# The compression's narrow products between the values' products: one at a time, two behind every three, from the fifth chunk on

## The chip, the cores and the metric

The program runs on one core of a Trainium2 chip, as one launch. The metric is the device time of the whole program in microseconds (us). Before the change the median of three runs is 3626.85 us (3621.54 to 3629.15). A core has a matrix engine (TensorE, PE in the rows), a vector engine (VectorE, DVE), an engine for activation functions and copies (ScalarE, ACT), a general engine (GpSimd, POOL) and one that issues transfers (SyncE, SP). Each works through its own list of instructions in the order of that list; an instruction waits until what it reads is there and the buffer it writes is free.

## The reference

Sequence 512, width 1024, fp32. The first block has two layers, each a feed-forward part, a mixer and a second feed-forward part; a second block (pooling and attention mixers, squared-ReLU MLPs, with a context of 256) follows. The change is in the mixer of the first block, which runs twice, once a layer:

```python
z = n @ mix_w_in[l]                      # queries, keys/values, gates, u and v
y_a = _nsa(q, k_cmp, v_cmp, k_sel, v_sel, k_win, v_win, gates, pe, w1, w2)
y_b = _gmlp(zuv, ln_g, ln_b, ws, bs)

def compress(t, j):                      # in _nsa: 31 windows of 32 positions
    blk = t[:, win_idx] + pe[j][None, None, :, None, :]
    h = jax.nn.silu(jnp.einsum('bnlgd,ldf->bngf', blk, w1[j]))
    return h @ w2[j]
...
kc = _rope(compress(k_cmp, 0), ccos, csin);  vc = compress(v_cmp, 1)
# o = gate0 * attention over kc/vc + gate1 * selected blocks + gate2 * window

def _gmlp(uv, ln_g, ln_b, ws, bs):
    u, v = jnp.split(jax.nn.gelu(uv), 2, axis=-1)
    v = _layernorm(v, ln_g, ln_b)
    ...                                  # chunks of 128 positions, 8 groups
    sv = jnp.einsum('gts,bnsgc->bntgc', w, v) + bs.T[None, None, :, :, None]
    return u * sv.reshape(B, S, GM_WIDTH)
```

## The kernel before

Dense products keep fp32 precision by splitting each operand into a high part and a rest: ScalarE makes the high part of a weight (`whi`, L98), VectorE or GpSimd the rest (`wlo`, L100), and three products are summed (`mm3`, L114 to L116). Weights arrive as raw tiles of 128 x 1024 in three buffers.

In `mix_body` the mixer goes as follows.

- **Queries and keys of group 0**: products (512 wide), rotation (`rotate`, L669 reads the product's PSUM buffer), and the split into high part and rest: `qs` (L688) on VectorE, `kk` by ScalarE (L699), VectorE (L701) and GpSimd (L702).
- **Values** (`values`): eight chunks k of the 1024 inputs, and for each chunk four blocks i of 128 tokens; each of these 32 places is one `mm3` with 280 columns (L114 to L116, `128x280`), into four PSUM buffers, two of the pool `s` and two of the pool `mm`.
- **Compression** (`compress(0)` for keys, `compress(1)` for values): 16 products each of 62 columns over the raw keys or values, `aux<-B,raw` at L761, the narrow products; behind them tanh, the product with w2 (L771 for keys, L786 for values), the rotation of the compressed key (L774 to L778, its sum is `kc`) and its transposition (L780).
- **gMLP, v** (`tok_proj`, L654 to L656, 256 wide, weights from `mix_gv`), gelu (L913, L915), layernorm (L925 to L935, result `vln`).
- **Attention**, group by group: scores against the compressed keys (L832, 16 products of 64 columns) and a softmax in `pcm` (L836); then scores (L815, L816, mask L869), softmax `p` (L873 to L882), transpositions (L886, L891), products with the values (L854, L855), and sums `yv` (L898, L899).
- **Queries and keys of group 1**, and the **spatial gating**: u (gelu), products `ws` x `vln` (L959).

`values` and `compress` are generators. The loop at L797 runs the values, which yield once per chunk, and from chunk `CMP_FROM` = 2 on adds `CMP_RATE` = 1.5 to an account, from which whole steps of the compression are taken; a step of the compression is four narrow products (it yields where q % 4 == 3). What remains runs behind the loop (`run_steps(cmp)`).

What is written so is not the last word on the order: a scheduler then lists each engine's instructions anew by its own estimates of when their operands are ready, within the limits of the pools' buffers. So gv products stand among the values and the attention, and products of group 1 (the fill in the text below) among the steps of the attention of group 0.

Of the kernel before, what the change touches and what calls it, by code (L numbers as in the profile page):

```python
# [32 lines left out]
GELU_A = 0.044715  # L33
GELU_B = 0.7978845608028654
WINDOWS = (2, 4, 8, 16)
CMP_FROM, CMP_RATE = 2, 1.5
BAND = 144
WEAVE = (2, 3, 3, 1.65, 3)

# [12 lines left out]
def build(tc, d, stop=99):  # L52
# [27 lines left out]
    def pc(name, off=0, n=8):  # L80
        o = PCOLS[name] + off
        return par[:, o:o + n]
# [5 lines left out]
    def psum(pool_=None, tag="mm"):  # L88
        return (pool_ or cur["mm"]).tile([128, 512], F32, name=tag, tag=tag)

    def wload(src, F=1024):
        raw = wraw_p.tile([128, 1024], F32, name="raw", tag="raw")
        SY.dma_start(raw[:, :F], src)
        return raw[:, :F]
# [8 lines left out]
    def wget(src, F=1024, eng=None):  # L103
        return wsplit(wload(src, F), F, eng)

    def split(hi, lo, src, eng=None):
        A.activation(hi, src, AF.Copy)  # L107
        (eng or V).tensor_tensor(lo, src, hi, op=OP.subtract)  # L108
# [4 lines left out]
    def mm3(ps, lh, ll, rh, rl, start, stop):  # L113
        T.matmul(ps, lh, rh, start=start, stop=False)  # L114
        T.matmul(ps, lh, rl, start=False, stop=False)  # L115
        T.matmul(ps, ll, rh, start=False, stop=stop)  # L116
# [70 lines left out]
    def modcols(mods, g, jsh, jsc):  # L187

        gs = small.tile([128, 8], F32, name="gs", tag="gs", bufs=4)
        V.scalar_tensor_tensor(gs, mods[:, jsc * 8:(jsc + 1) * 8], 1.0, g, op0=OP.add, op1=OP.mult)  # L190
        return gs, mods[:, jsh * 8:(jsh + 1) * 8]
# [239 lines left out]
    def run_steps(gen, n=None):  # L431
        if gen is None:
            return
        i = 0
        for _ in gen:
            i += 1
            if n is not None and i >= n:
                return

    def chain(*gens):  # L440
        for g in gens:
            yield from g
# [143 lines left out]
    def mixer(l, mods, pre, tail):  # L586
        with ExitStack() as st:
            mix_body(l, mods, pre, tail, st)

    def mix_body(l, mods, pre, tail, st):  # L590
# [14 lines left out]
        def t2(name, shape=(128, S)):  # L605
            return tmp.tile(list(shape), F32, name=name, tag="t2")
# [133 lines left out]
        def values(pss):  # L740
            for k0, kn in ((0, 3), (3, 3), (6, 2)):
                hi, lo = wget(d["mix_v"][l, :, k0 * 280:(k0 + kn) * 280], kn * 280)
                for kk in range(kn):
                    k = k0 + kk
                    w0, w1 = hi[:, kk * 280:(kk + 1) * 280], lo[:, kk * 280:(kk + 1) * 280]
                    for i in range(4):
                        sl = slice(i * 128, (i + 1) * 128)
                        mm3(pss[i][:, 0:280], nhi(k)[:, sl], nlo(k)[:, sl], w0, w1, k == 0, k == 7)
                    yield

        w2s = mc.tile([128, 2, HD], F32, name="w2", tag="w2")
        SY.dma_start(w2s, d["cmp_w2"][l].rearrange("j p e -> p j e"))
# [1 line left out]
        def compress(j):  # L754
            B, w2 = KV_BLOCKS[j], w2s[:, j]
            hp = psum(aux, "aux")
            hv = hp[:, 0:62].rearrange("p (g n) -> p g n", g=NG)
            for w in range(2):
                w1 = wload(d["cmp_w1"][l, j, w])
                for q in range(8):  # L760
                    T.matmul(hv, w1[:, q * 128:(q + 1) * 128], B[:, 8 * w + q, :, 0:NCMP], start=w + q == 0, stop=w * q == 7)  # L761
                    if q % 4 == 3:
                        yield
            z = hp[:, 0:62]
            th = mc.tile([128, 62], F32, name="zth", tag="zth")
            A.activation(th, z, AF.Tanh, scale=0.5)
            sv = mc.tile([128, 62], F32, name="sv", tag="sv")
            V.scalar_tensor_tensor(sv, th, 1.0, z, op0=OP.add, op1=OP.mult)
            if j == 0:
                kp = psum(aux, "aux")  # L770
                T.matmul(kp[0:62, 0:HD], sv, w2, start=True, stop=True)  # L771
                ta, tb, kc = t2("kt1", (62, HD)), t2("kt2", (62, HD)), t2("kc", (62, 2, HD))
                V.tensor_tensor(ta, kp[0:62, 0:HD], ropec[:, 0], op=OP.mult)
                V.tensor_tensor(tb.rearrange("p (j e) -> p j e", j=2),  # L774
                                kp[0:62, 0:HD].rearrange("p (j e) -> p j e", j=2)[:, ::-1, :],
                                ropec[:, 1].rearrange("p (j e) -> p j e", j=2), op=OP.mult)
                for e in range(2):
                    V.tensor_tensor(kc[:, e], ta, tb, op=OP.add)  # L778
                tp = psum(aux, "aux")
                T.transpose(tp[:, 0:62], kc.rearrange("p e d -> p (e d)"), ident[0:62, 0:62])  # L780
                tv = tp[:, 0:62].rearrange("p (g n) -> p g n", g=NG)
                split(KC[:, 0, :, 0:NCMP], KC[:, 1, :, 0:NCMP], tv)
            else:
                vp = psum(aux, "aux")
                for g in range(NG):
                    T.matmul(vp[0:NCMP, g * HD:(g + 1) * HD], sv[:, g * NCMP:(g + 1) * NCMP], w2,  # L786
                             start=True, stop=True)
                vf = t2("vf", (NCMP, NG, HD))
                V.tensor_scalar(vf, vp[0:NCMP, 0:128].rearrange("p (g e) -> p g e", g=NG), 0.5, None,
                                op0=OP.mult)  # L790
                split(VC[0:NCMP, :, 0], VC[0:NCMP, :, 1], vf)
            yield

        pss = [psum(s_p, "s") if i < 2 else psum() for i in range(4)]
        cmp = chain(compress(0), compress(1))
        acc = 0.0
        for k, _ in enumerate(values(pss)):  # L797
            if k >= CMP_FROM:
                acc += CMP_RATE
                run_steps(cmp, int(acc)) if acc >= 1 else None  # L800
                acc -= int(acc)
        for i in range(4):
            split(VV[:, i, :, 0], VV[:, i, :, 1], pss[i][:, 0:256].rearrange("p (c e) -> p c e", c=4))
            A.activation(gth[:, i], pss[i][:, 256:280], AF.Tanh, scale=0.5)
# [662 lines left out]
    with ExitStack() as st:  # L1467
# [3 lines left out]
        with ExitStack() as ist:  # L1471
# [29 lines left out]
            gs, _ = modcols(ml1, pc("g_mix_pre_2", 8), 0, 1)  # L1501
# [120 lines left out]
            for u in (0, 1, 4, 2, 3, 5):  # L1622
                own = first_tiles(u) if u < 2 else None
                pss = [x[:, 0:256] for x in own] if own else tok_proj(d["qkv"][u], u > 3)
# [222 lines left out]
```

## Time and profile before

| | |
|---|---|
| median of three runs | 3626.85 us |
| the profiled execution's own time | 3629.45 us |
| its span in the trace | 3627.7 us |
| instructions in the span | 44600 |
| mean granted TensorE clock, share of full | 0.979 |
| TensorE busy | 3472.6 us (96%) |
| VectorE busy | 2299.2 us (63%) |
| ScalarE busy | 1462.9 us (40%) |
| GpSimd busy | 476.0 us (13%) |

Busy shares are over the whole span. The granted clock is a share of full speed, 2.4 GHz; 0.5 is the lower level, 1.2 GHz. In rows of the timeline a matmul's start is the useful column: the matmuls are pipelined, so a row's duration overlaps the next one, and the step from start to start is what a product takes of the engine. The first mixer of the two lies at about 390 to 680 us, the second at about 1540 to 1830.

### The profile page before, as it was taken

To read this page: it belongs to the slowest core of one execution; us is meant where nothing else is said; L and a number is where in the kernel's file an instruction comes from. 1 tells how busy PE (TensorE), PEld (TensorE's weight loads), DVE (VectorE), ACT (ScalarE), POOL (GpSimd) and SP (SyncE) were. 2 spreads that over 40 slices of the span, in tenths; PEclk is the share of its full clock that TensorE was granted. 3 is DMA by queue.
4 is the path that set the end of the run, shared out by engine and by line. 5 is a ranking of instruction groups with operands and counts; after the bars stand their busy time and mean duration, and the time that the engine had idled before them with its cause. 6 is when DMAs were issued, how large, how long until landed. Compare 5 with 4: busy or idle time off the path is not lost.

```text
span 3627.7 us, 44600 instructions
## 1 busy us (share of the span) xinstructions
PE 3472.6 (96%) x16924; PEld 2861.7 (79%) x16924; DVE 2299.2 (63%) x3715; ACT 1462.9 (40%) x2487; POOL 476.0 (13%) x470
## 2 busy tenths in 40 slices
PE   7999999999999999999999999979999988989998
PEld 5788886788878888887688888868888877767886
DVE  8863677458753996378636966675445578654434
ACT  4222475433223422257624224654433435634232
POOL 4020113021000303022104020210000021130000
PEclk9999999999999999999999999989999999999999
DMA  6862221236862475231123763314444421013332
GB/s 237 287 235 92 95 77 48 69 103 240 292 210 91 156 244 171 88 109 51 44 88 133 248 234 99 108 56 134 128 130 127 133 66 59 1 47 99 97 96 70
DMA packets 140985, 461.55 MB, mean 127 GB/s; under 512 B 16869, under 2 KB 19297, under 8 KB 140641
## 3 DMA queue, kind: packets, MB, share of 16 engines
q1 hardware_dynamic: 140768, 458.69, 38.9%
q8 instruction: 133, 2.18, 0.2%
q14 instruction: 84, 0.68, 0.1%
HBM read 456.53 MB, written 2.10 MB: 126 GB/s over the span
## 4 chain that ended last, share of the span: by engine, by line
PE 63%; DVE 7%; ACT 2%; issue 1%; POOL 1%; DMA 1%; SPq 0%; DVEq 0%; ACTq 0%; POOLq 0%
PE mm L114 18%; PE mm L116 18%; PE mm L115 18%; DVE nt L200 1%; DVE wlo L100 1%; PE mm L324 1%; PE aux L1665 1%; PE aux L886 1%; DVE h L1108 0%; DVE n L206 0%; PE o L854 0%; ACT whi L98 0%; DVE ssum L150 0%; POOL shp L215 0%; PE o L115 0%
## 5 line engine op out<-in xcount | busy, mean ns | idle before, releaser
L98 ACT ACTIVATE whi<-raw 128x1024 fp32r<-128x1024 f32 (+2 forms) x636 | 619.3, 976 | 1469.1 <-PE mm L115 1075.0
L100 DVE TENSOR_TENSOR wlo<-raw,whi 128x1024 fp32r<-128x1024 f32 (+3 forms) x605 | 694.7, 1150 | 506.9 <-ACT whi L98 499.0
L114 PE MATMUL mm<-n,whi 128*128 128x512 f32 x2096 | 831.5, 397 | 14.2 <-ACT nt L202 9.2
L116 PE MATMUL mm<-n,wlo 128*128 128x512 f32 x2096 | 824.6, 394 | 4.3 <-DVE wlo L100 4.1
L115 PE MATMUL mm<-n,whi 128*128 128x512 f32 x2096 | 822.8, 393 | 0.4 <-DVE n L206 0.2
L114 PEld LDWEIGHTS mm<-n,whi 128*128 128x128 f32 x2096 | 395.8, 189 | 98.4 <-issue 11.3
L116 PEld LDWEIGHTS mm<-n,wlo 128*128 128x128 f32 x2096 | 395.3, 189 | 95.7 <-DVE wlo L100 7.3
L115 PEld LDWEIGHTS mm<-n,whi 128*128 128x128 f32 x2096 | 395.7, 189 | 85.2 <-DVE n L206 0.9
L423 DVE SCALAR_TENSOR_TENSOR junk<-adaw,crow 128x1024 f32<-128x1024 f32 x288 | 353.3, 1227 | 76.7 <-DMA adaw<-adaT 59.3
L114 PE MATMUL mm<-r,whi 128*128 128x512 f32 x976 | 385.5, 396 | 4.6 <-ACT r L254 3.1
L116 PE MATMUL mm<-r,wlo 128*128 128x512 f32 x976 | 385.1, 395 | 0.1
L115 PE MATMUL mm<-r,whi 128*128 128x512 f32 x976 | 382.3, 392 | 0.2 <-DVE r L108 0.2
L114 PEld LDWEIGHTS mm<-r,whi 128*128 128x128 f32 x976 | 183.6, 188 | 44.4 <-ACT r L254 4.0
L116 PEld LDWEIGHTS mm<-r,wlo 128*128 128x128 f32 x976 | 183.9, 188 | 43.0 <-DVE wlo L100 0.8
L115 PEld LDWEIGHTS mm<-r,whi 128*128 128x128 f32 x976 | 184.0, 189 | 41.6 <-DVE r L108 0.5
L114 PE MATMUL mm<-hid,whi 128*128 128x512 f32 x448 | 176.7, 394 | 0.0
L116 PE MATMUL mm<-hid,wlo 128*128 128x512 f32 x448 | 175.7, 392 | 0.0
L115 PE MATMUL mm<-hid,whi 128*128 128x512 f32 x448 | 174.7, 390 | 0.0
L563 DVE SCALAR_TENSOR_TENSOR h<-mm,hg,h 128x512 f32<-128x512 f32 x96 | 71.9, 749 | 118.5 <-PE mm L116 118.2
L150 POOL TENSOR_TENSOR ssum<-ssum,sq 128x512 f32<-128x512 f32 x27 | 40.6, 1504 | 778.2 <-ACT sq L149 778.2
L545 DVE TENSOR_TENSOR hd<-mm,sil 128x512 f32<-128x512 f32 x79 | 54.4, 688 | 116.0 <-PE mm L116 115.7
L108 DVE TENSOR_TENSOR ptl<-aux,pth 128x512 fp32r<-128x512 f32 x144 | 94.7, 684 | 43.8 <-ACT pth L107 43.2
(500 smaller groups left out, 5808.3 us busy)
## 6 DMA issues: line engine op xcount, KB each, us to landing
adaw<-adaT SPq DMA_DIRECT2D x240, 512.0 KB, 4.8
raw<-ffn_in SPq DMA_DIRECT2D x170, 512.0 KB, 4.6
raw<-mlp_in SPq DMA_DIRECT2D x96, 512.0 KB, 3.8
raw<-ffn_out SPq DMA_DIRECT2D x64, 512.0 KB, 4.3
raw<-mlp_out SPq DMA_DIRECT2D x64, 512.0 KB, 3.8
raw<-mlp_out SPq DMA_DIRECT2D x64, 256.0 KB, 2.9
raw<-ffn_out SPq DMA_DIRECT2D x32, 384.0 KB, 3.1
raw<-mix_zb SPq DMA_DIRECT2D x16, 512.0 KB, 3.6
```

Of the source, the lines that this page charges most:

```text
L98: A.activation(hi[:, :F], raw, AF.Copy)
L100: (eng or cur["lo"]).tensor_tensor(lo[:, :F], raw, hi[:, :F], op=OP.subtract)
L108: (eng or V).tensor_tensor(lo, src, hi, op=OP.subtract)
L114: T.matmul(ps, lh, rh, start=start, stop=False)
L115: T.matmul(ps, lh, rl, start=False, stop=False)
L116: T.matmul(ps, ll, rh, start=False, stop=stop)
L150: self.last = (eng or V).tensor_tensor(self.acc, self.acc, sq, op=OP.add)
L200: V.scalar_tensor_tensor(t, src[:, k], gs[:, k:k + 1], bc, op0=OP.mult, op1=OP.mult)
L324: T.matmul(self.pss[n], w[:, sl], x, start=k + e == 0, stop=k == DC - 1 and e == 2)
L423: V.scalar_tensor_tensor(junk, w, 1.0, cs[v], op0=OP.mult, op1=OP.mult, accum_out=mods[v][:, j * 8 + m:j * 8 + m + 1])
L545: V.tensor_tensor(hd, pss[1], sil, op=OP.mult)
L563: V.scalar_tensor_tensor(h[:, m], ps, hg[:, m:m + 1], h[:, m], op0=OP.mult, op1=OP.add)
```

## The change

The values yield after every `mm3`, so 32 times, and hand out the chunk's number; the compression yields after every narrow product; and from the chunk of index 4 on, two steps of the compression are taken after each `mm3`. The account goes. From L799 on, the new file's lines are 2 to 3 lower than the old one's.

```diff
-CMP_FROM, CMP_RATE = 2, 1.5
+CMP_FROM, CMP_RATE = 4, 2
...
                     for i in range(4):
                         sl = slice(i * 128, (i + 1) * 128)
                         mm3(pss[i][:, 0:280], nhi(k)[:, sl], nlo(k)[:, sl], w0, w1, k == 0, k == 7)
-                    yield
+                        yield k
...
                     T.matmul(hv, w1[:, q * 128:(q + 1) * 128], B[:, 8 * w + q, :, 0:NCMP], start=w + q == 0, stop=w * q == 7)
-                    if q % 4 == 3:
-                        yield
+                    yield
...
         cmp = chain(compress(0), compress(1))
-        acc = 0.0
-        for k, _ in enumerate(values(pss)):
+
+        for k in values(pss):
             if k >= CMP_FROM:
-                acc += CMP_RATE
-                run_steps(cmp, int(acc)) if acc >= 1 else None
-                acc -= int(acc)
+                run_steps(cmp, CMP_RATE)
```

In TensorE's order of before, a layer's 32 narrow products stand as a block of 8 at the start of the values, two blocks of 4 among them, and a block of 16 behind them. This is the stretch between the two blocks of 4, one whole chunk of the values (`n_3011`, `n_3012` are the normed input's high part and rest, `B` the raw keys or values with the positions' offsets):

```order
L761 MATMUL aux<-B,raw 128x62 x4
L114 MATMUL s<-whi,n_3011 128x280
L115 MATMUL s<-wlo,n_3011 128x280
L116 MATMUL s<-whi,n_3012 128x280
...
L114 MATMUL mm<-whi,n_3011 128x280
L115 MATMUL mm<-wlo,n_3011 128x280
L116 MATMUL mm<-whi,n_3012 128x280
L761 MATMUL aux<-B,raw 128x62 x4
```

And this is TensorE's order of the changed kernel, where the values' fifth chunk stands:

```order
L116 MATMUL s<-whi,n_3012 128x280
L761 MATMUL aux<-B,raw 128x62 x2
L114 MATMUL s<-whi,n_3011 128x280
L115 MATMUL s<-wlo,n_3011 128x280
L116 MATMUL s<-whi,n_3012 128x280
L761 MATMUL aux<-B,raw 128x62 x2
L114 MATMUL mm<-whi,n_3011 128x280
L115 MATMUL mm<-wlo,n_3011 128x280
L116 MATMUL mm<-whi,n_3012 128x280
L761 MATMUL aux<-B,raw 128x62 x2
```

The two blocks of 4 have become four pairs, each behind three products; the blocks of 8 and of 16 are as before.

At the end of the values TensorE had, before (`n_3011` and `n_3012` are the normed input's high part and rest, `kc__3197` the compressed keys, `qs_3235` the queries of group 0, `sv` the compression's hidden layer):

```order
L654 MATMUL mm<-whi,n_3011 128x256
L780 MATMUL aux<-ident,kc 128x62
L761 MATMUL aux<-B,raw 128x62 x16
L655 MATMUL mm<-wlo,n_3011 128x256
L656 MATMUL mm<-whi,n_3012 128x256
L654 MATMUL mm<-whi,n_3011 128x256
L655 MATMUL mm<-wlo,n_3011 128x256
L832 MATMUL s<-kc__3197,qs_3235 128x64 x8
L786 MATMUL aux<-w_3321,sv 31x64 x2
L832 MATMUL s<-kc__3197,qs_3235 128x64 x8
L656 MATMUL mm<-whi,n_3012 128x256
```

and has in the changed kernel (lines up to 3 lower):

```order
L116 MATMUL mm<-whi,n_3012 128x280
L779 MATMUL aux<-ident,kc 128x62
L761 MATMUL aux<-B,raw 128x62 x16
L829 MATMUL s<-kc__3197,qs_3235 128x64 x5
L785 MATMUL aux<-w_3321,sv 31x64 x2
L829 MATMUL s<-kc__3197,qs_3235 128x64 x11
L654 MATMUL mm<-whi,n_3011 128x256
L655 MATMUL mm<-wlo,n_3011 128x256
L812 MATMUL s<-kk_3268,qs_3235 128x128
```

No gv product stands between the values and the compressed scores any more; they have moved behind these, and two of them instead of ten stand ahead of the first score of the attention. On VectorE the first copy of the keys (L701) has moved ahead of the sum of the compressed key (L778); on ScalarE and GpSimd the copies of the keys have moved ahead of the first gv weights' parts.

Behind the attention of group 0, TensorE had before (`n_3011`, `n_3012` as above, `vln_4200` and `vln_4201` the normed v; the product that the gating interrupts is one for group 1):

```order
L116 MATMUL mm<-n_3011,wlo 128x512
L959 MATMUL mm<-ws,vln_4200 64x128 x2
L959 MATMUL mm<-ws,vln_4201 64x128 x2
L959 MATMUL mm<-ws,vln_4200 64x128 x2
L959 MATMUL mm<-ws,vln_4201 64x128 x2
L114 MATMUL mm<-n_3011,whi 128x512
```

and has in the changed kernel:

```order
L829 MATMUL s<-kc__3197,qs_4522 128x64 x7
L956 MATMUL mm<-ws,vln_4200 64x128
L114 MATMUL mm<-n_3011,whi 128x512
L115 MATMUL mm<-n_3012,whi 128x512
L956 MATMUL mm<-ws,vln_4200 64x128
L116 MATMUL mm<-n_3011,wlo 128x512
L114 MATMUL mm<-n_3011,whi 128x512
L956 MATMUL mm<-ws,vln_4201 64x128
L115 MATMUL mm<-n_3012,whi 128x512
L116 MATMUL mm<-n_3011,wlo 128x512
L956 MATMUL mm<-ws,vln_4201 64x128
```

The gating's first products stand singly among wide ones, and seven compressed scores of group 1 have come ahead of them. Of the 18 products of one group of 512 columns that stood inside the attention of group 0, two are left there; the other 16 stand behind it. Before the first score of group 1 stand 21 products of 512 columns where there were 16, and 11 instead of 13 between that score and the first transpositions.

On VectorE, ahead of that gating, before (`rp` is the rotation, `qs_4522` the queries of group 1):

```order
L669 TENSOR_TENSOR rp_4600<-mm,rope 128x512
L133 SCALAR_TENSOR_TENSOR rs_y<-rs_b,rs_y 128x4
L935 SCALAR_TENSOR_TENSOR vln_4200<-vln_4200,rs_y,lnb 128x512 x2
L935 SCALAR_TENSOR_TENSOR vln_4201<-vln_4201,rs_y,lnb 128x512 x2
```

and in the changed kernel:

```order
L688 SCALAR_TENSOR_TENSOR qs_4522<-rp_o,qs_4522 64x512
L132 SCALAR_TENSOR_TENSOR rs_b<-rs_a,vv_4480 128x4
L133 SCALAR_TENSOR_TENSOR rs_y<-rs_b,rs_y 128x4
L669 TENSOR_TENSOR rp_4646<-mm,rope 128x512
L932 SCALAR_TENSOR_TENSOR vln_4200<-vln_4200,rs_y,lnb 128x512 x2
L932 SCALAR_TENSOR_TENSOR vln_4201<-vln_4201,rs_y,lnb 128x512 x2
```

The last two instructions for the queries (L688) and the rotation of the keys (`rp_4646`) now stand ahead of the layernorm's last step, which is what the gating reads. Behind the last `yv` of the attention of group 0 VectorE has, ahead of this place, one more L913, three more L934, one more L915 and one more L925. Both layers have the same order.

## Rows read from the trace of the kernel before

**Rows 1.** The page's busy times: us, share of the span, instructions.

```profile
PE 3472.6 (96%) x16924; PEld 2861.7 (79%) x16924; DVE 2299.2 (63%) x3715; ACT 1462.9 (40%) x2487; POOL 476.0 (13%) x470
```

**Rows 2.** The chain that ended last, by engine, shares of the span.

```profile
PE 63%; DVE 7%; ACT 2%; issue 1%; POOL 1%; DMA 1%; SPq 0%; DVEq 0%; ACTq 0%; POOLq 0%
```

**Rows 3.** Windows: stretch, length, busy PE, PEld, DVE, ACT, POOL, PEclk, DMA, GB/s.

```profile
446.30:448.50 2.20, 2.20 (x11) 2.20 (x11) 2.20 (x3) 0.74 (x2) 2.20 (x2) 0.51 0.35 63
448.50:455.00 6.50, 6.50 (x54) 6.50 (x53) 4.90 (x7) 4.51 (x7) 1.30 (x2) 1.00 0.46 184
465.00:470.00 5.00, 5.00 (x29) 5.00 (x27) 2.35 (x9) 0.91 (x8) 1.66 (x2) 0.55 0.79 238
470.00:475.00 5.00, 5.00 (x26) 4.77 (x26) 2.39 (x8) 3.49 (x4) 2.15 (x1) 0.50 0.20 79
475.00:480.00 5.00, 5.00 (x29) 5.00 (x29) 3.73 (x6) 1.44 (x5) 2.55 (x2) 0.58 0.54 171
500.00:540.00 40.00, 39.80 (x249) 31.30 (x247) 32.73 (x74) 31.55 (x79) 2.83 (x4) 1.00 0.21 66
560.00:580.00 20.00, 15.53 (x82) 11.73 (x81) 17.39 (x22) 12.28 (x19) 10.44 (x8) 1.00 0.18 54
```

**Rows 4.** PE's waits, 560 to 620: waiting and releasing line, us, times, longest.

```profile
PE mm L114 <- DVE rp L669: 2.1, 1, 2.1
PE s L815 <- DVE pcm L836: 1.9, 1, 1.9
...
PE mm L959 <- DVE u L915: 1.1, 1, 1.1
...
PE mm L959 <- ACT qs L687: 0.7, 1, 0.7
```

**Rows 5.** Timeline of PE, second layer: start, us, instruction, idle before and releaser.

```profile
1609.40 0.38 PE L654 MATMUL mm<-whi,n 128*128 128x256 f32 x1 [0.71 <-ACT whi L98]
```

**Rows 6.** Timeline of PE, a block of four narrow products among the values.

```profile
453.31 1.00 PE L761 MATMUL aux<-B,raw 128*128 128x62 f32 x8
454.12 0.38 PE L114 MATMUL s<-whi,n 128*128 128x280 f32 x1
454.33 0.29 PE L115 MATMUL s<-wlo,n 128*128 128x280 f32 x1
454.46 0.29 PE L116 MATMUL s<-whi,n 128*128 128x280 f32 x1
```

**Rows 7.** Timeline of PE, behind the values.

```profile
462.93 0.27 PE L780 MATMUL aux<-ident,kc 62*128 62x62 f32 x1
463.12 4.91 PE L761 MATMUL aux<-B,raw 128*128 128x62 f32 x32
...
472.77 0.56 PE L656 MATMUL mm<-whi,n 128*128 128x256 f32 x1
...
478.94 0.40 PE L655 MATMUL mm<-wlo,n 128*128 128x256 f32 x1
```

**Rows 8.** The tile kk on VectorE: count, duration ns min/median/max, first and last start.

```profile
L701 DVE TENSOR_TENSOR kk<-rp_o,kk x2: 689/1553/2417, 463.1 to 465.6; 64x512 fp32r<-64x512 f32 x2
```

**Rows 9.** Timeline of PE, 24 products of 512 columns, the first and the last.

```profile
558.15 0.39 PE L114 MATMUL mm<-n,whi 128*128 128x512 f32 x1
...
563.41 0.40 PE L116 MATMUL mm<-n,wlo 128*128 128x512 f32 x1
```

**Rows 10.** Timeline of PE, the first transpositions of the attention of group 0.

```profile
483.43 0.65 PE L886 MATMUL aux<-ident,p 128*128 128x128 f32 x4 [1.34 <-DVE p L882]
```

**Rows 11.** Lines of VectorE, 495 to 575: busy us, mean ns, idle before.

```profile
L915 DVE SCALAR_TENSOR_TENSOR vln<-ge_a,mm 128x256 f32<-128x256 f32 x8 | 3.3, 408 | 0.6 <-ACT ge_a L914 0.6
L913 DVE TENSOR_TENSOR ge_a<-mm,ge_a 128x256 f32<-128x256 f32 x8 | 3.2, 419 | 0.1
L934 DVE SCALAR_TENSOR_TENSOR vln<-vln,mv,lng 128x512 f32<-128x512 f32 x4 | 2.9, 732 | 0.0
L925 DVE BATCH_NORM_STATS2 st<-vln 128x6 f32<-128x512 f32 x4 | 2.6, 670 | 0.0
```

## The prediction, on record before the changed kernel ran

> **What bounds the kernel now.** I read the page's shares first: TensorE is busy for 96% of the span, VectorE for 63% [rows 1], and the chain of work that ended last lies on TensorE for 63% and on VectorE for 7% [rows 2]. A change that only moves TensorE's work can therefore gain or lose three things: TensorE's own time (its clock, and what a change of shape between two products costs), waits that open or close, and the cover that a moved product gave to another engine. Next I read the windows of the first mixer [rows 3]. At 448.50 to 455.00, where narrow compression products stand in small blocks among the values' products, the granted clock is 1.00. It is 0.51 at 446.30 to 448.50, at the first block of narrow products. It falls to 0.55 at 465 to 470 and stays at 0.50 and 0.58 until 480, behind the block of sixteen, and TensorE is busy all that time, 5.00 of 5.00. At 500 to 540, inside the attention of group 0, TensorE is busy for 39.80 of 40.00 us, with VectorE at 32.73. At 560 to 580, around the gating and the start of group 1, it is busy for only 15.53 of 20.00, and VectorE for 17.39: there the kernel is bound by VectorE. The view of waits for 560 to 620 names them: 2.1 us on the rotation (L669), 1.1 on u (L915), 0.7 on qs (L687), and at the first scores of group 1 1.9 us on pcm (L836) [rows 4]. Those are the only waits of size near the edit. So the title's place, the values, has nothing to wait for; what can be won or lost is the clock behind the block, and what the new order does some 100 us later.
>
> **What the change does, part by part.** No arithmetic is added or removed. All numbers are for one layer; the second layer has the same order and the same waits, as its gv product shows [rows 5], so each counts twice.
>
> *The products themselves.* Of the 32 narrow products, the order keeps the first eight as a block at the start of the values, and the last sixteen as a block behind them. Only eight are moved: from two blocks of four to four pairs. A block of four (eight records) takes 0.81 us from its start to the next wide product (453.31 to 454.12), and the first wide product behind it takes 0.21 to the next start where a later one takes 0.13 (454.12, 454.33, 454.46) [rows 6]. So a return from narrow to wide costs 0.08 us, and two more of them +0.16. At the block of sixteen there were two returns to gv products (the block, then the compressed scores); now there is one, at a clock of about half: -0.16, and these two cancel.
>
> The transposition of the compressed key (L780, 462.93 [rows 7]) waits for VectorE, in whose queue the copy of the keys (L701) has moved ahead of the sum that it reads. The two copies of before take 0.69 and 2.42 us [rows 8]. The wait so added lies between 0 (the sum is ready first, as before) and +2.42. I take +0.3, about half of the short one: ScalarE's copy ahead of it has moved up too, and POOL now does its own copies of the keys before the first gv split, so that the two engines' work falls apart. Behind this transposition on TensorE are the block of sixteen and all the rest.
>
> *The clock.* The low stretch begins with the block of sixteen (463.12 for 4.91 us) and lasts past the compressed scores to at least 478.94 [rows 7]. From 472.77 on it holds wide products alone: 6.2 us at half clock, which would take 3.1 at the full one. The order now brings the wide products about 1 us sooner, since no gv products stand between the block and the compressed scores. If the clock comes back by as much earlier, -0.5. The bounds: -3.1 (all of that stretch at full clock), and +1.5 (it lasts 3 us longer at half clock). I take -0.5.
>
> By the Trainium skill, "TensorE: Matmul & The Clock Gate", section "What's actually happening", the clock follows how busy the array has been, and idling brings it down. The row does not bear that out in this form: at 465 to 470 the engine is busy 5.00 of 5.00 at 0.55. By the rule alone this term would be 0, and the sum higher by 0.5 a layer.
>
> *The attention of group 0.* Between its steps the program puts fill: gv products and a product of 24. Sixteen 512-wide products that ran inside now run behind it. They start 23 steps in 5.26 us (558.15 to 563.41 [rows 9]), 0.229 each, so 3.66 us of cover leave. If they were surplus cover, the attention ends 3.66 us sooner and nothing is lost; if every one of them covered a wait, it ends no sooner and 3.66 are lost. TensorE at 39.80 of 40.00 says that cover was enough, and VectorE at 32.73 of 40 that it has room [rows 3]. The only gap of its kind near the start is 1.34 us, before the first transpositions (483.43 [rows 10]). I take a third of that, +0.5 (bounds 0 and +3.66).
>
> *VectorE's chain to the gating.* Work of the gMLP that VectorE did under the attention now stands behind the last of the attention's sums: one more L913, three L934, one L915 and one L925, that is 0.42 + 3 x 0.73 + 0.41 + 0.67 = 3.7 us [rows 11]. Ahead of the gating on TensorE there are now the sixteen products as cover, 3.66. So 0.0. Bounds: +3.7, where they cover nothing because VectorE was already late; and -3.9, where the gating's products, now spread singly among wide products, no longer show the waits of 0.7, 2.1 and 1.1 [rows 4].
>
> *The start of group 1.* Before its first score stand five wide products more: they cover 5 x 0.229 = 1.14 of the wait of 1.9 on pcm [rows 4]. Between the first score and the first transpositions stand two fewer: +0.46. Together -0.7, bounds -1.1 and +0.5.
>
> The sum for a layer is 0.0 + 0.3 - 0.5 + 0.5 + 0.0 - 0.7 = -0.4, and twice that -0.8 us. The profiled execution took 3629.45 us, 2.6 above the median of 3626.85, so it would take 3628.6, and the median about **3626 us**: no change that can be told. What a measurement of this kernel can tell from no change is about 0.2%, 7.3 us. The bounds together reach from -8 to +12 a layer; not all ends of terms fall together, and the range below takes those that a mechanism ties.
>
> **Rivals.**
> *R1, faster: the spread gating hides its waits.* The single gating products now stand among wide ones, so TensorE has work while VectorE makes each vln. That gives -3.9 a layer in place of 0.0: -4.3, twice -8.6, **3618**. For it: 2.1 of the 3.9 is one wait on the rotation, which now stands ahead of the four L935 on VectorE. Against it: VectorE is busy 17.39 of 20.00 there, and its work has grown, so waits move rather than go.
> *R2, a little faster: the clock comes back with the wide products.* Then -3.1 in place of -0.5: -3.0 a layer, **3621**. For it: it came back within 2.2 us at 448.50. Against it: the sixteen narrow products and the compressed scores still stand in one run, longer than before, and 472.77 to 478.94 was dense and slow.
> *R3, slower: the attention is held by its own steps on ScalarE and VectorE.* Without the sixteen products TensorE waits there, 3.66 us a layer, and at the start of group 1 the five further products gain nothing, as the first score waits for VectorE in any case. That is -0.2 (the key's wait and the clock) + 3.66 + 0.46 = +3.9, twice +7.8, **3635**. It passes 0.2% once 3.4 of the 3.66 us come back as waits between 480 and 550. For it: VectorE and ScalarE are busy for 80% of that stretch, so there is little room. Against it: 39.80 of 40.00.
> *R4: the change does not do what it says.* In part that is so by the order already, since sixteen of the 32 still stand in one block; it is in the forecast.
>
> Chances: the forecast 0.52, R1 0.20, R2 0.10, R3 0.18. Faster by over 0.2%: most of R1, a part of R2 (it lies 1.5 us short) and of the forecast's own spread, 0.24. Slower by over 0.2%: two thirds of R3 and a little of the forecast, 0.16. Within: 0.60. The range that leaves out 2 in 10 goes past R1, for it could fall together with part of R2, and past R3: 3614 to 3637. The forecast's own range is 3621 to 3631.
>
> **What would show it.** Right: the pairs cost 0.08 us each at a clock of 1.00; the low stretch still begins with the block of sixteen and ends within a microsecond or two of where it did; at 490 to 545 no wait on p or ptl above 0.5 us; before the gating waits of 3 to 5 us in all on VectorE; the first score of group 1 waits for under 1 us on pcm. Wrong: waits of VectorE's that sum to over 3 us inside the attention of group 0 (R3), a gating without waits (R1), a clock of 1.00 before 472 (R2). The forecast as a whole is wrong if the difference is beyond 0.2%, or if the layers differ from one another.

## The result, and the profile after

The changed kernel is slower: 3645.42 us median of 11 runs (3635.35 to 3656.35) beside 3625.53 us for the kernel before in the same comparison, a ratio of 1.0060 (95% interval 1.0048 to 1.0072). The prediction was 3626 with a range of 3614 to 3637, so both its sign and its range missed.

Each run also gives the granted clock's mean over the span. One minus that mean, times the span, is the time lost if TensorE always had work at half clock: 92.1 us in the mean of the changed kernel's runs, 72.9 to 76.1 in the five sets of runs of before that went with the experiments. By this measure 16 to 19 of the some 20 us look like clock. It counts time at half clock in which TensorE had nothing to do as well; the account by mixer further down gives the clock a smaller part. Here is the page of after, which answers to [rows 1]:

```profile
PE 3479.4 (96%) x16924; PEld 2865.5 (79%) x16924; DVE 2308.5 (63%) x3715; ACT 1462.4 (40%) x2487; POOL 469.3 (13%) x470
```

TensorE is busy longer with the same 16924 instructions: that is a lower clock, not more work. The windows of after, cut along the stretches where the clock is low in the first mixer (columns as in [rows 3]):

```profile
467.50:477.70 10.20, 10.20 (x52) 9.97 (x51) 4.19 (x13) 3.41 (x9) 4.71 (x2) 0.50 0.53 168
484.50:491.40 6.90, 6.52 (x29) 5.81 (x29) 3.39 (x12) 3.18 (x12) 0.25 (x1) 0.51 0.10 39
501.60:505.00 3.40, 3.40 (x17) 3.22 (x16) 0.84 (x3) 2.36 (x7) 0.45 (x1) 0.50 0.39 154
576.70:583.50 6.80, 5.30 (x13) 2.38 (x12) 6.70 (x9) 3.79 (x6) 4.12 (x4) 0.50 0.00 0
```

The first stretch is the one that [rows 3] showed behind the block of sixteen, 13.7 us then and 10.2 now. The other three are new. Before, the windows 500 to 540 and 560 to 580 had a clock of 1.00 [rows 3], and so had 480 to 500:

```profile
480.00:500.00 20.00, 18.50 (x133) 15.59 (x132) 12.97 (x37) 13.44 (x45) 5.58 (x5) 1.00 0.10 37
```

The first two new ones start where a wait ahead of transpositions ends. The waits of TensorE in after, 440 to 560 and then 560 to 640 (line, releaser, us, times, longest; the second view answers to [rows 4]):

```profile
PE aux L883 <- DVE p L879: 5.3, 2, 3.3
PE aux L761 <- POOL B L725: 2.2, 1, 2.2
PE aux L779 <- DVE kc L777: 1.4, 1, 1.4
```

```profile
PE s L829 <- DVE qs L688: 3.2, 2, 2.6
PE mm L956 <- DVE vln L932: 1.5, 1, 1.5
PE aux L883 <- DVE p L879: 1.4, 1, 1.4
PE s L812 <- ACT p L870: 0.8, 1, 0.8
```

Two waits on p stand out: 3.34 us where [rows 10] had 1.34, and 1.94 us where there was none.

```profile
484.88 0.47 PE L883 MATMUL aux<-ident,p 128*128 128x128 f32 x1 [3.34 <-DVE p L879]
...
501.32 0.45 PE L883 MATMUL aux<-ident,p 128*128 128x128 f32 x2 [1.94 <-DVE p L879]
```

**Where the two waits come from.** VectorE's timeline ahead of each, in after:

```profile
480.06 2.22 DVE L841 TENSOR_TENSOR rsc<-rsc,gates 128x16 f32<-128x16 f32 x1
...
498.76 2.50 DVE L879 TENSOR_SCALAR p<-p,rs 128x256 f32<-128x256 f32 x1
```

And GpSimd's, in after:

```profile
473.66 2.36 POOL L100 TENSOR_TENSOR wlo<-raw,whi 128x1024 fp32r<-128x1024 f32 x1 [3.64 <-ACT whi L98]
479.88 2.37 POOL L100 TENSOR_TENSOR wlo<-raw,whi 128x1024 fp32r<-128x1024 f32 x1 [3.86 <-PE s L866]
...
498.76 2.36 POOL L100 TENSOR_TENSOR wlo<-raw,whi 128x1024 fp32r<-128x1024 f32 x1 [14.01 <-ACT whi L98]
```

The same two instructions of VectorE in the kernel before (L844 and L882 there), and ahead of them a subtraction (L838):

```profile
476.08 2.02 DVE L838 TENSOR_TENSOR pcm<-pcm,mxc 128x512 f32<-128x512 f32 x1
...
480.60 0.17 DVE L844 TENSOR_TENSOR rsc<-rsc,gates 128x16 f32<-128x16 f32 x1
...
494.86 0.34 DVE L882 TENSOR_SCALAR p<-p,rs 128x256 f32<-128x256 f32 x1
```

And GpSimd's splits before, the second and the third in one row:

```profile
472.85 4.70 POOL L100 TENSOR_TENSOR wlo<-raw,whi 128x1024 fp32r<-128x1024 f32 x2 [5.46 <-ACT whi L98]
...
489.00 2.39 POOL L100 TENSOR_TENSOR wlo<-raw,whi 128x1024 fp32r<-128x1024 f32 x1 [5.70 <-ACT whi L98]
```

GpSimd's splits make the rest of the gv weights (`wlo`). A product of 16 columns on VectorE takes 2.22 us instead of 0.17, and ends (482.28) when GpSimd's split ends (482.25). The scaling of p takes 2.50 instead of 0.34, and ends (501.26) just behind the fourth split (501.12). All that the transpositions need is queued behind these two on VectorE. Before, GpSimd's third split ran at 475.2 to 477.6 beside the subtraction (L838), which TensorE was not waiting for: VectorE was idle again, waiting for TensorE, at 479.7. The fourth ran at 489.0, clear of the scaling. The Trainium skill, "SBUF — State Buffer", section "Who interferes with whom", says that a VectorE instruction with two inputs in SBUF contends with a GpSimd instruction that reads SBUF, and calls the contention "an exclusive lock". The rows of L841 agree, 0.17 and 2.22. The scaling of p has one tensor and a column of factors as its inputs; that it is held up too is shown by its rows, 0.34 and 2.50.

In the first mixer the first transposition is no later for all this, counted from the first narrow product: 39.1 us, and 39.5 before. TensorE has 30 gv products ahead of it instead of 40, and the time so saved goes into the wait.

**Why the splits moved.** VectorE's order at the end of the values, in after: the keys' rest (L701) stands ahead of the sum of the compressed key.

```profile
463.34 0.21 DVE L773 TENSOR_TENSOR kt<-aux,ropec 62x64 f32<-62x64 f32 x1
463.47 0.41 DVE L108 TENSOR_TENSOR vv<-s,vv 128x256 fp32r<-128x256 f32 x1
464.01 0.68 DVE L701 TENSOR_TENSOR kk<-rp_o,kk 64x512 fp32r<-64x512 f32 x1
464.62 0.21 DVE L777 TENSOR_TENSOR kc<-kt,kt 62x64 f32<-62x64 f32 x1
```

On GpSimd the copies of the keys have moved ahead of the first gv split. They are not what holds up the third and the fourth: GpSimd is idle for 3.86 and 14.01 us ahead of these. The fourth starts when ScalarE has made the weight's high part (498.68). The third starts when its high part (479.80) and the mask product on TensorE that its row names (L866) have both just ended; which of the two it waited for is not shown. In ScalarE's new order both high parts stand behind exponentials of the attention (L870). ScalarE's high parts of the second and third gv weights, in one row, before:

```profile
471.67 1.99 ACT L98 ACTIVATE whi<-raw 128x1024 fp32r<-128x1024 f32 x2
```

And of the third and the fourth in after:

```profile
478.76 1.05 ACT L98 ACTIVATE whi<-raw 128x1024 fp32r<-128x1024 f32 x1
...
497.63 1.05 ACT L98 ACTIVATE whi<-raw 128x1024 fp32r<-128x1024 f32 x1
```

Counted from the first narrow product, the third split starts some 3 us later than before and the fourth some 8.

### The profile page after: what moved, and what is told of

Its sections match the earlier page's. It is cut to its first block, busy times and chain, and to the rows that moved or that the text cites. A ratio compares the mean times of both kernels' runs of the same rounds, so it can differ in the third digit from the quotient of the medians.

```text
span 3643.0 us, 44589 instructions
## 1 busy us (share of the span) xinstructions
PE 3479.4 (96%) x16924; PEld 2865.5 (79%) x16924; DVE 2308.5 (63%) x3715; ACT 1462.4 (40%) x2487; POOL 469.3 (13%) x470
## 4 chain that ended last, share of the span: by engine, by line
PE 79%; DVE 12%; DMA 4%; ACT 2%; issue 2%; POOL 1%; SPq 0%; DVEq 0%; ACTq 0%; POOLq 0%
PE mm L114 22%; PE mm L116 22%; PE mm L115 21%; DMA adaw<-adaT 3%; PE mm L324 2%; DVE junk L423 1%; DVE wlo L100 1%; PE aux L883 1%; DVE nt L200 1%; PE o L851 1%; DVE n L206 1%; PE o L852 1%; PE s L812 1%; PE s L324 1%; PE s L813 1%
## 5 line engine op out<-in xcount | busy, mean ns | idle before, releaser
L150 POOL TENSOR_TENSOR ssum<-ssum,sq 128x512 f32<-128x512 f32 x27 | 39.5, 1462 | 769.9 <-ACT sq L149 769.9
```

The source lines that it names most:

```text
L150: self.last = (eng or V).tensor_tensor(self.acc, self.acc, sq, op=OP.add)
```

## The experiments

Three theories stood at the start. C: the time is TensorE's clock, which falls behind longer waits. W: it is the waits themselves. P: it is the pairs of narrow products. A fourth, K, came out of the profiles of the first eight runs: GpSimd's splits stand beside steps of VectorE that TensorE waits for. Ratios are to the kernel before, which ran beside each.

**e1: the numbers alone.** The kernel before with `CMP_FROM, CMP_RATE = 4, 2`.

> Only the two numbers are changed (4, 2), the yields stay coarse: among the values the second eight narrow products stand as one block of eight instead of four pairs; behind the values TensorE's order is word for word that of the changed kernel. Theory C (the time is TensorE's clock, which falls behind the longer wait ahead of the first transpositions of the attention of group 0 and again at the gating): as the changed kernel, 3640 to 3650 us, ratio to before 1.005 to 1.007. Theory W (the waits themselves, not the clock): the same. Theory P (the narrow products standing in pairs among the wide ones cost the time): 3625 to 3631, ratio 1.000 to 1.0015.

3651.53 us, ratio 1.0079 (1.0062 to 1.0097), a little above the range of C and W. P falls: without any pair the loss is all there, with the same waits of 3.3 and 1.9 us. VectorE, ScalarE and GpSimd have the changed kernel's order here, instruction by instruction. So the loss comes with the two numbers and the order that the scheduler makes from them.

**e2 and e8: one chunk earlier, with pairs and as a block.** e2 is the changed kernel with `CMP_FROM, CMP_RATE = 3, 2`, e8 the kernel before with the same two numbers.

> The changed kernel with the pairs one chunk earlier (3 in place of 4). The pairs are all there, the compressed key is done twelve products earlier, and 15 gv products stand again ahead of the first score; but only 26 gv products stand between the first scores and the first transpositions of group 0 (30 before, 28 in the changed kernel). Theory P: 3640 to 3650, as the changed kernel. Theory W (late key, wait on VectorE at the end of the values, lost cover): about as before, 3622 to 3630. Theory C: it goes by the wait ahead of the first transpositions: if that is under 1.5 us, the clock stays at 1.00 from 484 to 510 and the time is 3620 to 3630; if it is 3 us or more, the clock falls behind it and the time is 3638 or more.

3621.20 us, ratio 0.9991 (0.9981 to 1.0001). In e2 the wait ahead of the first transpositions is 1.34 us, although only 26 gv products stand between the first score and these, where the changed kernel has 28. But ahead of that score e2 has 16 where the changed kernel has 2, so e2 alone does not tell whether the 3.3 us are a lack of cover; e7 does.

> The kernel before with the numbers 3, 2: the second eight narrow products stand as one block where the run from the fourth chunk has four pairs, and behind the values the order is that run's. If pairs cost or gain nothing: ratio to before as that run's, 0.998 to 1.001 (3616 to 3626). If each return from narrow to wide costs its 0.08 us: 0.5 us in all less. If the block of eight lets the clock fall at 455 to 460 as the first block does: 2 to 4 us more.

3623.52 us, ratio 0.9995 (0.9986 to 1.0004): pairs and a block of eight cannot be told apart in time.

**e3 and e4: the gaps filled with products that nobody reads.** e3 adds to the changed kernel, behind the fourth mask product; e4 does the same behind the last product of the keys of group 1 as well:

```diff
-                        T.matmul(s[:, sl], idbf, dmask, start=False, stop=True)
+                        last = T.matmul(s[:, sl], idbf, dmask, start=False, stop=True)
+                        if g == 0 and i == 0 and b == 0 and q == 3:
+                            with tc.issue_after(last.ins):
+                                for _ in range(20):
+                                    T.matmul(O, nhi(0)[:, 0:128], nhi(0), start=True, stop=True)
```

> The changed kernel with 20 further 512-wide products, whose result nobody reads, behind the last of the first four scores of group 0 and so ahead of the first transpositions, once a layer (4.6 us of work at full clock; 8 gv products and two heads' scores that stood there slip behind the transpositions, 1.7 us). Theory C: the wait of 3.3 us is covered, the clock stays at 1.00 through 484 to 492, 3.4 us a layer come back and 1.7 of the low stretch at 501, less the 1.7 that slipped: 3635 to 3641. Theory W: nothing comes back and the slipped work is added: 3646 to 3651.

3643.72 us, ratio 1.0057 (1.0041 to 1.0073). The window behind the filled gap in e3:

```profile
481.00:500.00 19.00, 16.32 (x115) 13.70 (x116) 12.37 (x29) 12.01 (x38) 3.48 (x4) 1.00 0.11 36
```

The wait is 0.63 us and the clock stays at 1.00 there, in both layers: so it is the gap that brings the clock down. But the 20 products are 4.6 us of work and the gap was 3.3, so the time gains nearly nothing. The expectation of C (3635 to 3641) was too low, that of W (3646 to 3651) too high.

> As the run before, and a further 20 such products behind the last keys' product of group 1, ahead of the gating, where TensorE waits 4.7 us in three pieces and the clock falls from 577 to 583; the gating's products stand there in a block of eight again. Theory C: the second low stretch goes too, 3.3 us a layer: 3628 to 3636. Theory W: the dense products there are cover for nothing but waits, 3644 to 3651.

3651.12 us, ratio 1.0069 (1.0052 to 1.0086): C's number missed altogether, and it is the upper end of W's. Over all runs the time lost at half clock is 81.7 us here, 86.7 in e3 and 92.1 in the changed kernel, so the clock does come back; the added products cost as much. Cover that is made of added work pays for itself at best.

**e5 and e6: products that start in the gap.** A copy of the maximum on GpSimd released 14 products in the first gap, and in e6 8 more in the second.

> The changed kernel with 14 further 512-wide products (4 rows of output, nobody reads them) that start when the maximum of the fourth head's first scores is there, so in the very gap of 3.3 us ahead of the first transpositions of group 0; two gv products slip behind it. Once a layer. They replace idle time one for one (14 x 0.229 = 3.2 us). Theory C (a gap costs clock on top of itself): the low stretch at 484 to 491 goes, 6.8 us x 0.46 = 3.1 us a layer come back: 3636 to 3642. Theory W (idle time costs what it lasts, the clock is incidental): 3645 to 3648, as the changed kernel.

> As the run before, and 8 more such products ahead of the transpositions of the second pair of blocks, where the changed kernel waits 1.9 us and the clock falls for 3.4 us at 502. Theory C: another 1 to 1.5 us a layer: 3633 to 3641. Theory W: 3645 to 3649.

3676.20 and 3679.00 us, ratios 1.0137 (1.0122 to 1.0153) and 1.0145 (1.0131 to 1.0159). Both theories missed, and the runs settle nothing. GpSimd made its copy late, TensorE waited 2.38 us for it, and the new tile shifted time in other stages too: in e5 the first mixer starts 5 us later than in the changed kernel.

```profile
487.33 4.97 PE L873 MATMUL o<-n,fx 128*4 128x512 f32 x14 [2.38 <-POOL fx L871]
```

**e7: two chunks earlier.** The changed kernel with `CMP_FROM, CMP_RATE = 2, 2`.

> The changed kernel with 2 in place of 4: the key's narrow products stand in pairs far ahead, the compressed key is done 33 products of the values before their end (no wait of 1.4 us for it), but from the first scores on the order is nearly that of the changed kernel: 26 gv products ahead of the first transpositions (28 there), and the sixteen 512-wide products stand behind the attention. Theory W1 (the late key and its wait are what costs): 3621 to 3629. Theory C: the gap and the low stretches in the attention stay: 3636 to 3648.

3638.56 us, ratio 1.0032 (1.0019 to 1.0044): about half the loss. The number lies in C's range, and W1 (the late key) missed: there is no wait for the key here, and a loss all the same. The first wait is 1.31 us, with 30 gv products ahead of the first transpositions as in the changed kernel; so the 3.3 us are no lack of cover. The second wait is still 1.94, and beside it the two scalings of p take 2.95 us (0.60 in the kernel before), under a GpSimd split at 498.64. This made K the theory.

**e9 to e12: the splits moved off GpSimd.** In e10 the third and the fourth gv weights' rest are made by VectorE; e9 moves the third alone, e11 is the same edit as e10 on the kernel before, e12 on e2.

```diff
-        def tok_proj(src):
+        def tok_proj(src, eng=(None, None)):
...
-                hi, lo = wget(src[:, k4 * 1024:(k4 + 1) * 1024])
+                hi, lo = wget(src[:, k4 * 1024:(k4 + 1) * 1024], eng=eng[k4])
...
-            for i, ps in enumerate(tok_proj(d["mix_gv"][l, c])):
+            for i, ps in enumerate(tok_proj(d["mix_gv"][l, c], (V, V) if c else (None, None))):
```

> The changed kernel with the third gv weights' rest (wlo) made by VectorE instead of GpSimd; the others stay on GpSimd. Theory K (in the changed kernel GpSimd's third split, 479.88 for 2.37 us, stands beside VectorE's small product rsc x gates, which takes 2.22 instead of 0.17 and holds up all that the first transpositions wait for): that small product takes about 0.2 again, the wait ahead of the first transpositions falls from 3.3 to 1.0 to 1.8 us, and the clock no longer falls at 36 to 43 us after the first narrow products; per layer 2 us of wait and 3.1 us of clock: 3633 to 3638. Rival (the wait comes from the order on TensorE, from fewer gv products ahead of the transpositions): the wait stays at 3 us and the time at 3643 to 3649.

3633.47 us, ratio 1.0028 (1.0016 to 1.0040). VectorE in e9, and the transpositions that it releases:

```profile
477.65 0.17 DVE L841 TENSOR_TENSOR rsc<-rsc,gates 128x16 f32<-128x16 f32 x1
477.74 1.22 DVE L100 TENSOR_TENSOR wlo<-raw,whi 128x1024 fp32r<-128x1024 f32 x1
```

```profile
481.34 0.66 PE L883 MATMUL aux<-ident,p 128*128 128x128 f32 x4 [1.19 <-DVE p L879]
```

The small product takes 0.17 us again, though VectorE now makes a split of 1.22 us itself, and the wait falls from 3.34 to 1.19. The second wait goes as well, since the fourth split now stands at 490.54. The edit also changed TensorE's order: four gv products more stand ahead of the first transpositions, some 0.5 us of work, and the gating's products stand together again.

> The third and the fourth gv split on VectorE. Theory K: the wait of 1.9 us ahead of the second pair's transpositions (GpSimd's fourth split, 498.76, beside VectorE's scaling of p, 2.96 us where it took 0.60 before) goes as well, with its 3.4 us at half clock: 3627 to 3634, and the rest to the kernel before is the gating's. Rival: 3643 to 3649.

3633.85 us, ratio 1.0027 (1.0017 to 1.0036), like e9, and at the upper end of what was expected.

> The same edit on the kernel before, where GpSimd's splits stand beside steps that nobody waits for. Theory K: nothing to win, VectorE gets 2.4 us a layer more: 3622 to 3630, ratio 0.999 to 1.0015. Rival (VectorE simply splits better than GpSimd): a gain like the one in the run before, 3610 or less.

3624.36 us, ratio 1.0005 (0.9995 to 1.0016). The edit is no gain of its own. So what e9 and e10 gave back, about half of the loss, came with the two collisions: some 4 us less of wait in each mixer, and the clock behind it. What the new order of the gating gave is not separated from that.

> The run from the fourth chunk (3, 2) with the same edit, as a version that may be faster than both kernels. Theory K: about that run's time, ratio to before 0.997 to 1.000.

3619.74 us, ratio 0.9986 (0.9977 to 0.9995): 0.14% ahead of the kernel before, as e13 and e15 below are, and not to be told from e2 without the edit.

**e13 and e14: what is left.** In e10 the gating's order is again that of before, and TensorE's waits are no longer in sum: some 12 and 11 us in the two mixers, some 13 in each before. What is left of the loss goes with the clock: 90.2 us by the measure above, where before's runs beside it have 76.1. e13 is e10 with the keys' rest of group 0 on GpSimd; e14 is e7 with both splits moved.

```diff
-                    V.tensor_tensor(kk[own, b, 1], kf[own], kk[own, b, 0], op=OP.subtract)
+                    (V if g else G).tensor_tensor(kk[own, b, 1], kf[own], kk[own, b, 0], op=OP.subtract)
```

> The run with both splits on VectorE, and besides the keys' rest of group 0 (L701) made by GpSimd, so that VectorE's sum of the compressed key is not held up. The sixteen narrow products and the sixteen compressed scores still stand in one piece on TensorE; gv products ahead of the first score are eleven. If what is left of the loss (0.27%) is the wait for the compressed key: the wait of 1.4 us a layer goes and the time is that of the kernel before, 3622 to 3629. If it is the clock behind the undivided narrow products: 3630 to 3638 as without this edit.

3618.83 us, ratio 0.9987 (0.9978 to 0.9997), some 3 us below the lower of the two ranges. Without the late key all of the rest comes back, and the measure of the clock is 72.3, though the sixteen narrow products and the compressed scores still stand in one run. At that run in the second layer, where e10 has its longest low stretch (17.1 us; 3.4 in the first layer), first e10 with the key late, then e13:

```profile
1608.00:1626.00 18.00, 17.31 (x83) 17.04 (x84) 7.88 (x26) 8.34 (x20) 5.93 (x4) 0.53 0.33 117
```

```profile
1610.00:1626.00 16.00, 13.80 (x113) 12.81 (x112) 11.18 (x32) 10.75 (x29) 10.47 (x8) 1.00 0.54 164
```

> The run from the third chunk (2, 2) with both splits on VectorE: no wait for the compressed key, and nine products of the values stand between the sixteen narrow products and the compressed scores. Without the edit it took 1.0032 of before. If GpSimd's fourth split beside VectorE's scaling of p was what it lost: 0.999 to 1.001 (3621 to 3629). If the loss lies elsewhere in that order: 1.002 or more.

3626.36 us, ratio 1.0009 (0.9999 to 1.0019): with the fourth split off GpSimd the second wait is gone, and with it most of what e7 lost.

**e15 and e16: one edit alone, and its control.** e15 is the changed kernel with only the edit of the keys' rest, e16 the kernel before with it.

> The changed kernel with one edit alone: the keys' rest of group 0 (L701) made by GpSimd, the splits left where they are. VectorE's sum of the compressed key comes earlier; from the first transpositions of the attention on, TensorE's order is again that of the kernel before, the gating's too, and GpSimd's third split moves against VectorE's chain. If the chain of causes is late key, hence copies and splits shifted, hence GpSimd's splits beside VectorE's steps, hence gaps and half clock: all goes, 3615 to 3627, ratio 0.998 to 1.001. If the two collisions stay, whatever the key does: 3632 or more.

3621.65 us, ratio 0.9989 (0.9979 to 0.9999). VectorE's order at the end of the values, and its small product, in e15:

```profile
464.37 0.20 DVE L773 TENSOR_TENSOR kt<-aux,ropec 62x64 f32<-62x64 f32 x1
464.50 0.41 DVE L108 TENSOR_TENSOR vv<-s,vv 128x256 fp32r<-128x256 f32 x1
464.83 0.34 DVE L777 TENSOR_TENSOR kc<-kt,kt 62x64 f32<-62x64 f32 x2
...
478.45 0.17 DVE L841 TENSOR_TENSOR rsc<-rsc,gates 128x16 f32<-128x16 f32 x1
```

```profile
PE aux L883 <- DVE p L879: 2.4, 2, 1.3
...
PE aux L779 <- DVE kc L777: 0.5, 1, 0.5
```

> The same edit on the kernel before, whose order on TensorE it leaves as it is. If GpSimd is simply the better place for that step, a gain as in the run with both edits: 3619 or less, ratio 0.9985 or less. If the edit matters only where the compressed key is late: ratio 0.999 to 1.001.

3625.73 us, ratio 0.9999 (0.9991 to 1.0008). The edit is worth nothing where the key is not late. e16 leaves all of TensorE's products in the order of before. In its profiled execution the stretch that stood at half clock for 13.7 us before ran at full clock, in both layers; the first:

```profile
465.50:479.70 14.20, 12.38 (x101) 11.27 (x100) 10.18 (x28) 8.31 (x27) 11.15 (x8) 1.00 0.58 185
```

So the first cause is shown: the place of one line, an instruction of 0.68 us that stands ahead of the compressed key's sum on VectorE. With that line on GpSimd the change costs nothing. What the 0.68 us do by themselves is not separated from the lists that the scheduler then makes anew for all engines: in e15 ScalarE's third high part stands ahead of the attention's exponentials again (473.94), and GpSimd's third split right behind it (475.08), clear of the small product. And e7 shows that a split can come to stand in a bad place without a late key.

## Why the prediction was wrong, point by point

- **The pairs** (cost of a return, cancelled to 0): right. e8 and e2, and e1 and the changed kernel, show no cost.
- **The wait for the compressed key** (+0.3 a layer): the number was right, by luck. Counted from the first narrow product the transposition starts at 19.33 us (465.11 less 445.78) where it was 19.00 (462.93 less 443.93). But the wait that I priced is 1.37 us; a gv product, with a wait of 0.7 on its weight, that stood just ahead of the transposition before stands there no longer. What failed is the step behind it: I priced the moved copies of the keys only by this delay. That GpSimd's copies moved ahead of the first gv split I used as a point in favour ("so that the two engines' work falls apart"), and did not follow the third and the fourth split, with ScalarE's high parts, to what then stood beside them on VectorE. Rows 8 showed the price of such a meeting, 2.42 beside 0.69 us, and I used it as a bound for one instruction in one place.
- **The clock** (-0.5, bounds -3.1 and +1.5): the step that cost most. Half clock held for 30.7 us of the first mixer instead of 17.1. I gave every wait its own length and no more, and looked for the clock only behind the block of sixteen. In the profiled execution of before that stretch began at 465.5, some 2.4 us into the block, and it is not fixed by the order. In e16 all of TensorE's 16924 products stand in the order of before, and the clock was 1.00 over that stretch in both layers. So one execution's profile does not tell what an order costs by the clock; the means over all runs do better. In the first mixers of 16 profiled executions (all but e5 and e6), from the first narrow product to the first update of h, the length less TensorE's waits and added products lies along one line, 316.3 us + 0.45 x the time at half clock, to within 1.5 us. So 13.6 us more at half clock are 6.1 us, and the waits are 2.6 longer (15.8 and 13.2): 8.7 together beside a measured 7.6. The clock took more than the waits that led to it.
- **The attention of group 0** (+0.5, bounds 0 and +3.66): the size was wrong, and the mechanism too. The sixteen products were surplus cover, as I said, as far as e14 shows: twelve of them stand behind the attention there, and its longest wait inside is 1.3 us. But the last product of the changed kernel's attention of group 0 starts 3.2 us later, counted from the first narrow product (555.77 less 445.78, and 550.74 less 443.93), although 3.66 us of fill had left: some 6.8 us went into the waits and the low stretches on the way.
- **VectorE's chain to the gating and the start of group 1** (0.0 and -0.7): the waits add up to 6.9 us (3.2 + 1.5 + 1.4 + 0.8) where that whole view of before has 9.0, so the sum of waits here fell by more than forecast. The clock fell instead: 6.8 us at 0.50 from 576.7.
- **The rivals**: R3 had the sign and the place, the attention held by its own steps on VectorE; its sign, waits of over 3 us there, came (5.3). Its price, +7.8, was less than half of what came, because it held no clock, and its reason, the missing cover, is refuted by e7. R1 and R2 did not come; the 2.2 us in which R2 saw the clock come back at 448.50 are the length of a window, and the stretch itself lasted 3.4 us.
- **Both layers alike**: the waits are (3.34 and 3.45 us at the first transpositions), the low stretches not quite: the first mixer takes 7.6 us more up to its first update of h, the second 7.2.

Left open: whether the key's wait of 1.4 us ahead of the narrow run costs the clock by itself. The traces speak for it. In all 16 mixers with that wait (the changed kernel, e1, e3 to e6, e9 and e10) the clock fell between 20 and 28 us after the first narrow product, for 3.4 to 17.1 us. Of the 20 others, where TensorE waits at most 0.72 us right there, four were at half clock in that stretch, both of the profiled execution of before among them. But e13, which takes the wait away and gets the time back, also has nine gv products more ahead of the first score than e10.

## What to carry to other kernels

When a small edit moves an instruction on VectorE or GpSimd, follow each later instruction of the one to what stands on the other at that time, and ask who waits for it: a short instruction on a critical chain can take as long as the long one beside it. Follow also what releases the long one, here ScalarE's high parts. In this kernel a gap on TensorE cost its length and then, where the clock fell behind it, 0.45 us for every microsecond at half clock. Before filling a gap with added work, look for the instruction that opens it: here one line moved to another engine did what 20 products could not.

## What was not expected of the hardware

- A 128x16 product on VectorE took 2.22 us beside a GpSimd subtraction of 2.37 us, and 0.17 without it.
- Behind the gaps of 3.3 and 3.4 us ahead of the first transpositions, the clock fell to 0.50 for 6.8 us in all four mixers that had one (the changed kernel's and e1's); with the gap filled to 0.5 or 0.6 us (e3, e4) it did not fall there. Of 23 mixers with gaps of 1.2 to 1.6 us at that place it fell for 3.4 us in 16, for 6.8 in one, and in six not at all, both of the kernel before among them.
- TensorE's clock also fell while the engine was busy throughout, 10.20 of 10.20 us at 0.50, over narrow products and compressed scores; in e13 and e15 the same products ran at 1.00.
- The spread between the 11 runs of the changed kernel is mostly clock: the time and the time lost at half clock go together (correlation 0.96). In the other sets of 11 runs or more the correlation is 0.5 to 0.9; the mean clock is known to three decimals only, 3.6 us of this measure a step.
